# Re-ordering a memory-to-memory quadrant swap: one DMA engine per neighbouring row, steps of 4 MB, one queue

## The chip, the cores and the metric

The kernel runs on one core of a Trainium2 chip. The metric is the device time of one execution in microseconds (us). "Before" is the tuned kernel, "after" the changed one. A ratio is the mean time of one kernel's fast runs over the mean time of the other's fast runs in the same rounds, so it is not quite the ratio of the medians that are quoted with it. An interval is a 95% interval.

Some words: DMA (direct memory access) engines are the 16 units that move the data. A transfer is what one instruction orders; it goes into a queue and is carried out in packets, here one contiguous piece by one engine. It has landed when all its packets are written, which a semaphore, a counter that can be waited for, reports. On a profile page each digit of the DMA line is the busy share of the engines in one fortieth of the span, in tenths (9 is 90% or more), and the GB/s line is the rate in the same fortieths.

## The reference

```python
"x": np.random.randn(8192, 8192).astype(np.float32)     # 256 MB
return np.fft.ifftshift(x)
```

With even sizes this swaps the quadrants: the upper left one with the lower right one, the upper right one with the lower left one. No value is computed. A row is 32 KB, half a row 16 KB, a quadrant 4096 half rows.

## The kernel before

```python
STEP = 8
...
    dims = [[STEP * C, hr // STEP], [1, hc]]
    for c in range(STEP):
        for col in (0, hc):
            for eng, r0, h in ((nc.sync, 0, col), (nc.scalar, hr, hc - col)):
                eng.dma_start(
                    out=bass.AP(out.tensor, out.offset + (r0 + c) * C + h, dims),
                    in_=bass.AP(x.tensor, x.offset + (hr - r0 + c) * C + hc - h, dims),
                )
```

There are 32 transfers of 8 MB, straight from memory to memory: 512 half rows each, every eighth row of a quadrant. A transfer is split over 16 DMA engines, 32 rows each, so the engines stand 8 MB apart and each walks in steps of 256 KB. Two queues, the sync engine's and the scalar engine's, each get 16 transfers.

## Time and profile before

| | before |
|---|---|
| time, median of 3 | 811.38 us (811.26 to 811.44) |
| span of the first profile | 821.3 us |
| half-row packets of 16 KB | 16,384, mean 801 ns in that profile |
| fastest packets | 611 ns |

The profiled execution of 821.3 us does not belong to the timed ones of 811.4 us. A later set of runs offers an explanation: of five chips on record four give about 811 us, but one gave 822.47 us for this very kernel (median of 9, 821.90 to 823.20), and the first profiled execution took 823.08 us.

To read such a page: there are no compute rows worth looking at. What matters is the busy line (are there holes?), the rate line (is there one regime or several?) and the packet durations in the trace (how long does 16 KB keep one engine?).

### The profile page before, as it was taken

What the parts mean: (1) busy time and instruction counts of PE and PEld (TensorE: products, weight loads), DVE (VectorE), ACT (ScalarE), POOL (GpSimd) and SP (SyncE); (2) the same over time, 40 slices, a digit from 0 to 9 for tenths busy, and PEclk for the clock granted to TensorE, in tenths of its full rate; (3) what the DMA queues carried; (4) which work ended last, traced back from release to release, by engine and by line L of the source; (5) the groups of instructions that cost most, each with busy time, mean ns of one, the idle gap of its engine ahead of it and who ended that gap; (6) DMA issues with size and microseconds to landing.
All of it is one profiled execution on the core that took longest, in us unless ns stands there. A gap on an engine that the chain in (4) does not pass through costs nothing. (4 is left out here: it accounts for less than half of the span.)

```text
span 821.3 us, 77 instructions
## 1 busy us (share of the span) xinstructions
POOL 0.2 (0%) x4
## 2 busy tenths in 40 slices
POOL 0000000000000000000000000000000000000000
DMA  9999999999999999999999999999999999999998
GB/s 304 325 328 333 326 325 330 321 329 330 325 330 330 327 328 333 329 330 330 328 328 327 334 325 330 326 326 328 331 329 330 326 332 326 328 324 333 326 328 298
DMA packets 16896, 268.44 MB, mean 327 GB/s; under 512 B 512, under 2 KB 512, under 8 KB 512
## 3 DMA queue, kind: packets, MB, share of 16 engines
q1 hardware_dynamic: 8448, 134.22, 50.2%
q10 hardware_dynamic: 8448, 134.22, 49.7%
HBM read 268.44 MB, written 268.44 MB: 654 GB/s over the span
## 5 line engine op out<-in xcount | busy, mean ns | idle before, releaser
L51 POOL MEMSET const-bfloat16-1.0<- 128x1 bf16 x1 | 0.1, 103 | 0.0
L51 POOL MEMSET const-uint8-127<- 128x1 uint8 x1 | 0.1, 102 | 0.0
L51 POOL MEMSET const-float32-0.0<- 128x1 f32 x1 | 0.1, 99 | 0.2 <-issue 0.2
L51 POOL MEMSET const-float32-1.0<- 128x1 f32 x1 | 0.1, 99 | 0.0
## 6 DMA issues: line engine op xcount, KB each, us to landing
out_dram<-in_x_dram ACTq DMA_DIRECT2D x16, 8192.0 KB, 204.3
out_dram<-in_x_dram SPq DMA_DIRECT2D x16, 8192.0 KB, 204.1
```

The source lines that it names most:

```text
L51: nc = _bacc.Bacc("TRN2", target_bir_lowering=False, num_devices=1)
```

## The change

The intent is to keep the 16 engines out of each other's way: at any moment they work on 16 neighbouring rows, one each, and move on together by 128 rows (4 MB). Eight passes with other residues fill a quadrant. All transfers go through one queue.

```diff
-STEP = 8
+ENGINES = 16
+POSITIONS = 8
...
-    dims = [[STEP * C, hr // STEP], [1, hc]]
-    for c in range(STEP):
+    stride = POSITIONS * ENGINES
+    dims = [[C, ENGINES], [stride * C, hr // stride], [1, hc]]
+    for r0 in (0, hr):
         for col in (0, hc):
-            for eng, r0, h in ((nc.sync, 0, col), (nc.scalar, hr, hc - col)):
-                eng.dma_start(
-                    out=bass.AP(out.tensor, out.offset + (r0 + c) * C + h, dims),
-                    in_=bass.AP(x.tensor, x.offset + (hr - r0 + c) * C + hc - h, dims),
+            for p in range(POSITIONS):
+                row = p * ENGINES
+                nc.sync.dma_start(
+                    out=bass.AP(out.tensor, out.offset + (r0 + row) * C + col, dims),
+                    in_=bass.AP(x.tensor, x.offset + (hr - r0 + row) * C + hc - col, dims),
                 )
```

Three things change at once: which engine touches which row, the number of queues, and the order of the quadrants.

## The prediction

> **What bounds the kernel now.** The kernel has no arithmetic: it copies four quadrants of a 256 MB matrix from memory to memory. So I read the page from the DMA side only: first the busy line and the rate line in 40 slices, then the queue totals, then the issues, then who waits on the issuing queues.
>
> ```profile
> DMA  9999999999999999999999999999999999999998
> GB/s 304 325 328 333 326 325 330 321 329 330 325 330 330 327 328 333 329 330 330 328 328 327 334 325 330 326 326 328 331 329 330 326 332 326 328 324 333 326 328 298
> DMA packets 16896, 268.44 MB, mean 327 GB/s; under 512 B 512, under 2 KB 512, under 8 KB 512
> ...
> q1 hardware_dynamic: 8448, 134.22, 50.2%
> q10 hardware_dynamic: 8448, 134.22, 49.7%
> HBM read 268.44 MB, written 268.44 MB: 654 GB/s over the span
> ```
>
> The reader is to see three things. The 16 DMA engines are busy in every slice, so there is no gap to close: time can only come out of how long one packet takes. The rate is flat, so there is one regime and not several stages. And each byte is counted twice at the memory: 268.44 MB read and the same written, 654 GB/s together.
>
> The 512 small packets are completion writes (32 transfers by 16 engines); the other 16,384 are half rows of 16 KB. The trace keeps start, duration and queue of each. Their mean duration is 801 ns and their sum over 16 engines 820 us, so packets fill the engines from first to last. Their distribution is the most telling fact: over a quarter stand at 611 ns (25th percentile 611, median 773, 90th 1046, 99th 1298). So 611 ns, 16,384 B at 26.8 GB/s per engine, is the pace of an engine that nothing delays, and the mean packet spends 190 ns over that. All 1,024 packets of each engine at 611 ns would be 626 us; the difference to 820 is delay in the memory or on the way to it.
>
> The issues are not the limit:
>
> ```profile
> out_dram<-in_x_dram ACTq DMA_DIRECT2D x16, 8192.0 KB, 204.3
> out_dram<-in_x_dram SPq DMA_DIRECT2D x16, 8192.0 KB, 204.1
> SPq L33 <- DMA out_dram<-in_x_dram: 133.8, 12, 50.6
> ```
>
> 204 us from issue to landing is eight transfers' worth: one takes 818 / 32 = 25.6 us of the engines' time, and eight semaphores are in rotation, four per queue. The 133.8 us on the third line are the sync queue waiting for one of its semaphores to come free, with several transfers still queued. The earliest issues, which met empty rings, took 0.6 to 0.9 us against the 25.6 us that a transfer lasts. Issue is 30 times faster than it has to be.
>
> One more view matters, the rate in chosen stretches (columns: microseconds, GpSimd, clock, DMA share, GB/s):
>
> ```profile
> 5.00:13.00 8.00, 0.00 (x0) 1.00 1.03 360
> ...
> 21.00:40.00 19.00, 0.00 (x0) 1.00 1.01 329
> ...
> 400.00:410.00 10.00, 0.00 (x0) 1.00 1.02 334
> ```
>
> In the first 8 us after the start-up the kernel moved about 350 to 360 GB/s. In the packet records these are ten rounds in which all 16 engines run in step, each packet 715 to 880 ns, none at 611, a new round every 744 ns on average (262,144 B / 744 ns = 352 GB/s). Then the engines fall out of step, durations spread from 611 to 1,500 ns, and the rate settles at 329. So contention among the 16 streams, not the total alone, costs the last 7%.
>
> **What the Trainium skill says.** "HBM Reference", section Specifications (TRN2), gives about 716 GB/s for a memory domain. The trace agrees with it as a ceiling: 654 GB/s over the span is 91% of it, and the in-step stretch, 2 x 352 = 704, is 98%. "DMA: Bandwidth & Descriptors", section Why a DMA increments its semaphore by 16 and not by 1, says that a transfer is split over the largest number of engines up to 16 that divides its slowest dimension. The trace agrees as far as it can: 16 completions per transfer (256 small packets per queue, 16 transfers). The same page, section Latency and other measured facts, reports that copies of tiles with rows of 16 KiB at a pitch of 4 or 8 MiB ran at 103 GB/s where padded ones had 214, and calls aliasing of lock-stepped streams an inference. This trace does not agree simply: neighbouring engines are now 8 MB apart and yet reach 91% of the ceiling. The same page, section Issuing engines are not separate DMA queues, says that a second issuing engine saves only issue time; the trace has that at 0.6 to 0.9 us.
>
> **The change part by part.**
>
> 1. Which engine touches what. Before: a transfer's slowest dimension is 512 rows at 8 rows (256 KB) pitch, split over 16 engines by 32 rows each. Engines are 32 x 256 KB = 8 MB apart, and each walks in steps of 256 KB. After: the slowest dimension is 16 neighbouring rows, so engines are 32 KB apart and each walks 32 rows in steps of 128 rows = 4 MB. Bytes, packet size (16 KB) and number of packets stay: 16,384. Cost by count: none. Its effect is all in the mean packet, 801 ns now. At 744 ns (the in-step stretch) the engines would need 1,024 x 744 = 762 us in place of 820; that is 58 us in the profiled run, 7%. This is the most I expect: it is also 98% of the skill's ceiling.
>
> 2. One queue. 32 transfers still; all from the sync engine. Issue: 32 x 0.9 = 29 us at most, spread over 800 us, all hidden. Three transfers per queue went out before an issue stalled at the start, so a single queue should hold some 3 x 25 = 75 us of work ahead. One queue alone can feed the engines: the first rounds of the trace are the sync queue's alone, and their packets took 611 and 662 ns. No gain, no loss by itself. What it does change is that at one time only one quadrant is read and one is written; today two pairs are interleaved packet by packet.
>
> 3. Order of quadrants. Now one queue writes left half rows while the other writes right half rows, so both halves are read and written at once. After, for 16 transfers at a stretch only one half row is read and only the other written (16 KB apart within the 32 KB row). If the memory spreads 16 KB pieces unevenly this could help or hurt; no view tells.
>
> Sum: 0 of issue, 0 of bytes, between -58 us and an unknown positive amount from the memory. I take a quarter to a third of the possible gain, about 15 us.
>
> **The rivals.** (a) The memory is the bound whatever the order: 654 of 716 GB/s with reads and writes mixed is already high, and the short in-step stretch is a start-up effect (writes lagging reads). For it: the rate is flat over 800 us through very different row positions, and the mean packet by position within a transfer hardly moves (748 to 850 ns, without a trend). Then 800 to 820 us. (b) Aliasing of steps: if each engine's own 4 MB step is what the skill's 103 GB/s come from, and not the distance among engines, the kernel slows; halved it would be 1,600 us, but milder forms, 850 to 950, are likelier, since 16 engines now lie in 16 different places of half a megabyte. Against it: padding by 4 KiB cured the skill's case, which spreads the streams in the low address bits, as 32 KB between engines does here. (c) The neighbours stay out of each other's way at any time, as no two engines ever share the low bits of a row number within a pass: the in-step rate holds for the whole run. 811.38 x 329 / 352 = 758 us. (d) The single queue leaves bubbles between packets: against it, the 611 ns packets of the first rounds.
>
> **Range and chances.** (a) is the likeliest single course, some 40%; (c), wholly or in part, some 35%; (b) and (d) together some 25%. Middle: 796 us, 811.4 less the 15 above. The range of 8 in 10 runs from a nearly full gain, 760, to a mild slowdown, 850. Chances: faster by over 2% (under 795) 0.37, within 2% 0.38, slower 0.25.
>
> **What would show it.** Step 1 is right if the mean of the 16 KB packets falls below 801 ns towards 744 and the rate line rises from 327 towards 350; wrong if the spread of packet durations stays as it is (a) or its upper tail grows beyond 1,300 ns (b). Step 2 is right if all packets stand on one queue, the busy line keeps its nines and landing stays near eight transfers' worth; holes in the busy line would show (d). Step 3 shows as a jump in the rate line halfway through each half of the span, where the column changes. The prediction fails most badly if the memory punishes a 4 MB step as the skill's tiles were punished.

## The result, and the profile after

| | before | after |
|---|---|---|
| time, median of 3 | 811.38 us (811.26 to 811.44) | 819.18 us (819.11 to 821.43) |
| ratio | | 1.0105 (1.0079 to 1.0132) |

The time hardly moves: the kernel is 1% slower, with an interval that leaves out 1.00. Executions over 1.5% slower than the fastest of the same kernel are left out of the means. These are the lines of the page of after that answer to those that the prediction shows of before:

```profile
DMA  9999999999999999999999999999999999999998
GB/s 300 331 326 333 330 337 330 331 330 332 325 333 331 333 324 333 329 331 330 329 326 338 331 327 327 328 334 332 327 330 339 326 329 333 326 325 334 332 326 292
DMA packets 16896, 268.44 MB, mean 328 GB/s; under 512 B 512, under 2 KB 512, under 8 KB 512
...
q1 hardware_dynamic: 16896, 268.44, 99.3%
HBM read 268.44 MB, written 268.44 MB: 657 GB/s over the span
...
out_dram<-in_x_dram SPq DMA_DIRECT2D x32, 8192.0 KB, 107.7
```

All packets stand on one queue; the busy line has kept its nines; the rate line is as flat as before, with no jump where the half row changes. From issue to landing it is now 107.7 us, some four transfers' worth. Semaphores are not the reason: the trace shows eight in rotation in both kernels. What changed is how much waits in the queues. On one queue the first three issue instructions took 0.6 to 0.7 us, but the median of all 32 is 24.6 us, about the time of one transfer. So the sync engine stands in the issue itself, presumably until there is room in the queue (argued from these times), with about four transfers under way. Two queues had eight. Engines that are always busy do not notice.

There is a trap here. This page says 657 GB/s and the first page of before says 654, as if the change had gained. The two pages come from different executions, and the timed runs say the opposite. So I ran both kernels again on one chip. The first fence is before, the second after:

```profile
GB/s 307 335 332 332 334 329 336 334 332 332 333 336 332 334 334 333 328 335 336 333 333 333 334 331 331 332 330 333 333 332 334 336 331 336 333 329 334 333 334 299
DMA packets 16896, 268.44 MB, mean 331 GB/s; under 512 B 512, under 2 KB 512, under 8 KB 512
...
HBM read 268.44 MB, written 268.44 MB: 663 GB/s over the span
```

```profile
GB/s 302 328 333 327 327 329 324 334 334 333 329 336 335 325 331 334 323 335 331 328 334 327 335 322 339 327 335 332 334 327 331 327 330 334 328 329 327 331 336 286
DMA packets 16896, 268.44 MB, mean 329 GB/s; under 512 B 512, under 2 KB 512, under 8 KB 512
...
HBM read 268.44 MB, written 268.44 MB: 657 GB/s over the span
```

Now the order is right: 663 GB/s before, 657 after. The packet records say where the difference sits. The mean packet is 786.3 ns before and 792.8 ns after; times 1,024 packets per engine that is 6.7 us, and the spans differ by 816.8 - 809.9 = 6.9 us. The floor of 611 ns has not moved; the upper tail has grown (95th percentile 1,059 to 1,134 ns, 99th 1,206 to 1,378). So in this pair the loss is a little more waiting inside packets, over the whole run, and nothing is left for issue or for the ends. The mean alone is not sharp enough to rest on: in the profile of b1_pairing below, a kernel that is nearly as slow as after, it is only 788.8 ns, and the rest lies between the packet records. The upper tail is the steadier mark, as will be seen.

### The profile page after: what moved, and what is told of

Its sections match the earlier page's. It is cut to its first block, busy times and chain, and to the rows that moved or that the text cites. A ratio compares the mean times of both kernels' runs of the same rounds, so it can differ in the third digit from the quotient of the medians.

```text
span 817.3 us, 77 instructions
## 1 busy us (share of the span) xinstructions
POOL 0.2 (0%) x4
## 6 DMA issues: line engine op xcount, KB each, us to landing
out_dram<-in_x_dram SPq DMA_DIRECT2D x32, 8192.0 KB, 107.7
```

## The experiments

The theory of the prediction (call it C) was that contention among the 16 streams takes 7% from the copy and that a better row order wins some of it back. Its main rival (M) was that the memory bounds reads and writes together, whatever the order. For the 1% of loss there were four suspects: the single queue (Q), the 4 MB step (S), engines on neighbouring rows (N), the order of half rows (H).

### Noise, and the queue alone

Four kernels ran on one chip. The first is before itself.

> The kernel before against itself, to size the noise. If the 811.4 us and the 823 us of its profiled execution are two samples of one spread, its runs here scatter between 811 and 823 and the ratio's interval is about 1% wide around 1.00. If the profile itself adds the 1.4%, the timed runs stay within 0.1% of 811.4 and only the profiled one is at 823.

Measured: 811.58 us (811.45 to 812.04) against 811.27 us, ratio 1.0004 (0.9992 to 1.0016). A ratio of 1.01 is thus far outside the noise. The profiled execution took 811.72 us, so profiling adds nothing; the guess that the profile costs 1.4% is dead.

The second is after, repeated.

> The changed kernel again on the same chip. Theory M (the memory bounds both orders alike): ratio 1.00 to 1.01, mean packet within 2% of before's. Theory L (a real loss of 1% from the new layout or the single queue): ratio 1.008 to 1.013 again, with an interval that leaves out 1.00.

Measured: 819.37 us (818.51 to 821.29), ratio 1.0103 (1.0089 to 1.0116). The loss is real.

The third undoes everything but the queue:

```diff
-            for eng, r0, h in ((nc.sync, 0, col), (nc.scalar, hr, hc - col)):
+            for eng, r0, h in ((nc.sync, 0, col), (nc.sync, hr, hc - col)):
```

> Only the queue part of the change: the rows of before, all 32 transfers on the sync engine's queue. Theory Q (the single queue costs the 1%): ratio 1.01, as the changed kernel. Theory M: ratio within 0.5% of 1.00; busy line keeps its nines and landing falls from 204 to some 105 us as in the changed kernel, since four transfers are in flight.

Measured: 811.69 us (810.48 to 811.78), ratio 1.0004 (0.9991 to 1.0016), mean packet 787.6 ns. The single queue costs nothing. Q is out.

The fourth keeps the new rows but gives neighbouring passes to two queues in turn:

```diff
-                nc.sync.dma_start(
+                (nc.sync, nc.scalar)[p % 2].dma_start(
```

> Only the row part of the change: 16 neighbouring rows, 4 MB steps, neighbouring passes on the sync and the scalar engine's queues in turn. Theory Q: the time of before, ratio 1.00. Theory that the 4 MB steps cost it: ratio 1.01 as the changed kernel. Theory M: within 0.5% of 1.00.

Measured: 822.73 us, ratio 1.0142 (1.0109 to 1.0174), with a wide scatter (817.69 to 828.71). The loss goes with the rows, not with the queue, and two passes side by side may make it larger (the intervals of the two ratios overlap). Why the scatter is wide I did not find out.

### Which part of the new row order

All four of the next kernels use one queue. The first takes the quadrants in before's order:

```diff
-    for r0 in (0, hr):
+    for p in range(POSITIONS):
+        row = p * ENGINES
         for col in (0, hc):
-            for p in range(POSITIONS):
-                row = p * ENGINES
+            for r0, h in ((0, col), (hr, hc - col)):
```

> The rows of the changed kernel, but the order of quadrants of before: transfers alternate between the two quadrant pairs, so both half rows are read and written within every 50 us. Theory H (reading one half row and writing the other for 16 transfers costs the 1%): ratio to before 1.000 to 1.003. Theory S (the 4 MB step) and theory N (engines on neighbouring rows): ratio 1.008 to 1.014 as for the changed kernel.

Measured: 818.54 us, ratio 1.0085 (1.0071 to 1.0098). H explains little or nothing of it.

The second makes the step small, 512 KB, and keeps the neighbours:

```diff
-    dims = [[C, ENGINES], [stride * C, hr // stride], [1, hc]]
+    dims = [[C, ENGINES], [ENGINES * C, hr // stride], [1, hc]]
...
-                row = p * ENGINES
+                row = p * (hr // POSITIONS)
```

> 16 neighbouring rows at a time as in the changed kernel, but each engine steps by 512 KB, a plain sweep through the quadrant. Theory S: back to before, 1.000 to 1.003. Theory N: 1.010 as the changed kernel. Theory H: 1.010 as well.

Measured: 817.00 us, ratio 1.0065 (1.0053 to 1.0078). Most of the loss stays (b1_pairing, with neighbours and 4 MB steps on the same chip, has 1.0085, and the two intervals overlap).

The third makes the step large, 16 MB, in transfers of 2 MB:

```diff
-POSITIONS = 8
+POSITIONS = 32
```

> The changed kernel with steps of 16 MB: 8 rows per engine and transfer, 128 transfers of 2 MB. Theory S: the loss is as large or larger, 1.010 to 1.03, and the 99th percentile of the packets rises over the changed kernel's 1378 ns. Theory N and H: 1.010, with the same packets. If the smaller transfers cost anything it shows as holes in the busy line.

Measured: 816.45 us, ratio 1.0058 (1.0044 to 1.0072). A larger step does not make it worse, which speaks against S.

The fourth keeps the 4 MB step and parts the engines, eight rows (256 KB) from each other:

```diff
-    dims = [[C, ENGINES], [stride * C, hr // stride], [1, hc]]
+    dims = [[POSITIONS * C, ENGINES], [stride * C, hr // stride], [1, hc]]
...
-                row = p * ENGINES
+                row = p
```

> Steps of 4 MB as in the changed kernel, but the engines 8 rows (256 KB) apart instead of on neighbouring rows. Theory S: 1.010 or more. Theory N: 1.000 to 1.003. Theory H: 1.010.

Measured: 811.15 us (810.59 to 811.37), ratio 0.9995 (0.9982 to 1.0007); the 99th percentile of the packets is back at 1,188 ns. This kernel has the 4 MB step, the single queue and the new order of half rows, and no loss. So N is the cause: the engines stand on neighbouring rows. On the chips of 811 us the 99th percentile agrees in every profile of a correct copy in 16 KB pieces without restarts: 1,338 to 1,381 ns in the six with neighbouring rows (both of after, a4, b1, b2, b3), 1,188 to 1,206 in the four without (a1, a3, b4 and d2 below). That the loss is 0.6% with steps of 512 KB and 16 MB and 0.9 to 1.0% with 4 MB stays unexplained.

### How far apart is far enough, and is it the reads or the writes

```diff
-    dims = [[C, ENGINES], [stride * C, hr // stride], [1, hc]]
+    dims = [[2 * C, ENGINES], [stride * C, hr // stride], [1, hc]]
...
-                row = p * ENGINES
+                row = p // 2 * 2 * ENGINES + p % 2
```

> The changed kernel with the engines two rows (64 KB) apart instead of one. If only direct neighbours disturb each other: ratio to before 0.998 to 1.002. If the loss fades with distance: about 1.005. If 64 KB is as bad as 32 KB: 1.009 to 1.012.

Measured: 810.73 us (810.51 to 811.56), ratio 0.9994 (0.9982 to 1.0006). With the engines on every second row the 1% is gone. The loss does not fade out over a longer distance: it is there at 32 KB and gone at 64 KB.

Two kernels use the near rows on one side only and rows 256 KB apart on the other. Their outputs are wrong, which doesn't matter for the times.

```diff
+    near = [[C, ENGINES], [stride * C, hr // stride], [1, hc]]
+    far = [[POSITIONS * C, ENGINES], [stride * C, hr // stride], [1, hc]]
...                                   # reads near, writes far; and the mirror
+                rrow, rdims, wrow, wdims = p * ENGINES, near, p, far
```

> One queue, 4 MB steps; the 16 engines read neighbouring rows (32 KB apart) but write rows 256 KB apart, a wrong result on purpose. If neighbouring reads cause the loss: ratio to before 1.007 to 1.012. If neighbouring writes do: 0.998 to 1.002. If both share: near 1.005.

> The mirror: reads 256 KB apart, writes on neighbouring rows, a wrong result on purpose. If neighbouring writes cause the loss: 1.007 to 1.012. If neighbouring reads do: 0.998 to 1.002. If both share: near 1.005.

Measured, on the slower chip where before itself takes 822.47 us: reads near 825.11 us, ratio 1.0031 (1.0017 to 1.0044); writes near 827.61 us, ratio 1.0064 (1.0051 to 1.0076). Both sides share, the writes with about twice the weight, and 0.31% + 0.64% is nearly the whole 1.0%. After itself was not run on this chip, so that the two losses add up to its loss is argued, not shown.

### Is there a faster regime to be had

First the ceiling. Two kernels move the same 16,384 pieces of 16 KB one way only, between memory and on-chip buffers. Their outputs are wrong, which doesn't matter for the times.

```diff
# reads only
+    pool = ctx.enter_context(tc.tile_pool(name="sb", bufs=8))
...
+                    t = pool.tile([P, hc], mybir.dt.float32)
+                    nc.sync.dma_start(out=t[:], in_=bass.AP(x.tensor, ..., dims))
# writes only: one tile t, to all half rows
+                    nc.sync.dma_start(out=bass.AP(out.tensor, ..., dims), in_=t[:])
```

> Only the reads: all half rows into on-chip buffers, almost nothing written to memory, so the result is wrong on purpose. Same 16,384 pieces of 16 KB. Theory M (memory reads and writes together are the bound, some 665 GB/s): the packets stand at the engines' own pace, 611 ns, and the time is about 1024 x 0.611 + 8 = 634 us. Rival R (the reads alone are already limited at some 330 GB/s): about 811 us.

> Only the writes: one on-chip tile written to all half rows, a wrong result on purpose. Theory M: packets at 611 ns, about 634 us. Rival W (writes alone are limited at some 330 GB/s, and the reads ride along): about 811 us.

Measured: 639.04 us (638.75 to 639.27) and 640.89 us (640.83 to 640.96), mean packets 615 and 617 ns. The rate lines, reads first, then writes:

```profile
GB/s 373 429 429 428 428 429 428 428 428 428 428 428 428 428 428 428 430 430 432 429 429 427 428 429 429 428 428 430 428 428 428 428 429 428 428 428 428 428 429 332
```

```profile
GB/s 328 427 427 427 427 427 427 427 427 427 427 427 427 427 427 427 427 427 427 427 427 426 427 428 427 427 427 428 427 430 428 427 427 429 428 427 427 427 428 385
```

The reader is to see lines without a ripple: alone, neither side is delayed much, and both run close to the 611 ns of the fastest packets of the copy. Only together, at 2 x 331 = 662 GB/s, does waiting appear. (These two runs also move between memory and on-chip buffers instead of memory and memory, in transfers of 2 MB with the engines 2 MB apart; that this alone changes nothing was not tested. So it is not shown whether the memory itself or the path to it sets the 662 GB/s.)

Then the start. The prediction had read ten quick rounds at the start of the trace as a regime that contention ends. This kernel starts all engines together 32 times, with before's rows and one queue:

```diff
+    sem = ctx.enter_context(nc.semaphore())
+    with tc.tile_critical():
...
+                    ).then_inc(sem, 16)
+                    n += 16
+                    nc.sync.wait_ge(sem, n)
```

> The rows of before on one queue, with a wait for each transfer's landing before the next is issued, so all 16 engines start in step 32 times. Prediction's own reading (the in-step stretch is a faster regime that contention ends): each restart gives some 10 rounds at 744 ns and no repayment, so the busy time of a transfer falls by 0.4 us and more against 25.2 us, and the whole is 811 + 32 x (2 to 3 us of empty pipes). Rival (start-up effect, reads running ahead of writes, repaid at once): ten fast rounds, then rounds above 800 ns, and the sum over a transfer is no less than in steady flow. Either way the time is some 880 us; the packet records tell them apart.

Measured: 874.85 us, ratio 1.078 (1.0764 to 1.0796). The busy line has the holes of 31 restarts:

```profile
DMA  9989998889988899888999899998899898999988
...
q1 hardware_dynamic: 16896, 268.44, 91.5%
```

The waits of the sync queue in the same run (who, for whom, us in total, times, longest):

```profile
SPq L36 <- DMA out_dram<-in_x_dram: 827.3, 31, 26.9
```

The sync queue stands 26.9 us for a landing at the longest, in place of queueing ahead. Worked out from the packet records: sort a transfer's 512 packets by start and take every sixteenth; the steps between these, averaged over the 32 transfers, are

```
round      1-5  about 1030, 683, 606, 609, 635 ns
round      6-12 about 719 741 743 741 742 742 754 ns
round     13-20 about 775 792 845 830 825 839 856 820 ns
round     21-31 about 780 767 804 814 783 789 796 789 805 752 800 ns
```

All 32 transfers have the same quick stretch, about 740 ns per round in rounds 6 to 12 (the stretch that the prediction built on), and in all 32 it is followed at once by slow rounds: rounds 13 to 20 take 823 ns on average (802 to 845 in the single transfers), more than the 786 ns of steady flow (the run on one queue, above); rounds 6 to 20 together average 784 ns. So this stretch is no regime that could last, and it is repaid.

The still quicker rounds before it are not repaid in this list: all 31 steps add up to 24.0 us, and 31 x 786 ns would be 24.4. The mean packet says the same, 780.1 ns against 787.6. That lies between the two readings of the expectation: 0.24 us less busy time per transfer, where the prediction's own reading asked for 0.4 and more, and the rival's for none. But each start has its cost too. The first packets take 1,119 ns on average, and from first packet to last end a transfer takes 25.57 us here, against 805.5 / 32 = 25.17 us in steady flow. By starting anew nothing is won. What is filled in the quick rounds and emptied later no record shows; that reads run ahead of writes is only argued.

### Is 811 us a floor for this copy

Whole rows, halves not swapped: the same bytes in half as many pieces. Its output is wrong, which doesn't matter for the time.

```diff
+    dims = [[STEP * C, hr // STEP], [1, C]]
```

> Whole rows of 32 KB moved between the upper and lower half, without swapping left and right, a wrong result on purpose: the same bytes in half as many pieces, and no half rows. Theory M: within 0.5% of 811 us. Rival (half rows leave the memory something to gain): below 795 us.

Measured: 812.64 us (812.35 to 813.50), ratio 1.0015 (1.0002 to 1.0028). The mean packet of 32 KB takes 1,578.6 ns, 789 per 16 KB. Longer pieces win nothing.

Pieces of 4 KB, with the engines 256 KB apart:

```diff
+    W = 1024
-    dims = [[POSITIONS * C, ENGINES], [stride * C, hr // stride], [1, hc]]
+    dims = [[POSITIONS * C, ENGINES], [stride * C, hr // stride], [1, W]]
+                for w in range(0, hc, W):
```

> The best order so far (engines 256 KB apart, 4 MB steps, one queue), each half row cut into four pieces of 4 KB in four transfers. Theory M (the sum of memory traffic is the bound): within 1% of 811 us, mean packet near 197 ns. Rival (the delay is one collision per piece or the piece's size sets it): clearly different, by over 2%.

Measured: 894.92 us (883.00 to 904.80), ratio 1.0947 (1.0907 to 1.0986); its profile fell in a slow run, so the rate is only roughly read from it:

```profile
DMA  9999999999999999999999999999999999999997
GB/s 285 320 308 315 289 295 310 287 312 284 298 317 281 315 289 302 315 286 311 287 301 313 295 310 288 295 317 286 316 283 305 311 287 317 287 302 313 288 311 244
```

The expectation of M was missed. The engines are busy all through, yet the rate swings between 281 and 320. More than half of the packets take 159 ns (four make 636, hardly over 611), but a tenth take 396 ns and more. The number of transfers is not the reason: b3_step_16m has 128 of 2 MB as well, and lost only its 0.6%. So the 811 us hold for pieces of 16 and 32 KB, not for this copy in 4 KB pieces. Whether the size of the pieces does it, or that an engine now jumps 4 MB after every 4 KB, was not separated.

### Can the place of the streams matter more than 1%

Before's rows on one queue, but each engine reads its first half row 32 times. Its output is wrong, which doesn't matter for the time.

```diff
-    dims = [[STEP * C, hr // STEP], [1, hc]]
+    odims = [[32 * STEP * C, 16], [STEP * C, 32], [1, hc]]
+    idims = [[32 * STEP * C, 16], [0, 32], [1, hc]]
```

> The copy on one queue with the rows of before, but each engine reads its first half row 32 times, a wrong result on purpose. Reads then touch 16 pieces per transfer instead of 512. If the order and place of the reads set the delay, the time falls clearly below 811 us, towards 762 or 634. If the path or the total of traffic sets it, it stays within 1% of 811.

Measured: 1960.75 us (1939.73 to 1972.52), ratio 2.41.

```profile
DMA  9999999999999999999999999999999999999999
GB/s 134 136 138 134 140 137 133 136 136 138 137 135 137 139 138 134 138 142 133 132 143 136 139 135 139 134 135 136 139 133 137 135 138 135 138 133 136 139 140 132
```

Neither expectation foresaw this. The busy line is as full as ever at less than half the rate, which is the best lesson on that line: busy is not fast. The same with the engines on neighbouring rows:

```diff
-    idims = [[32 * STEP * C, 16], [0, 32], [1, hc]]
+    idims = [[C, 16], [0, 32], [1, hc]]
```

(and the rows of the output as in after).

> The repeated reads again (each engine reads one half row 32 times, a wrong result on purpose), but with the engines on neighbouring rows instead of 8 MB apart. If reads 8 MB apart collide with each other, the time falls from 1961 us to about 811. If repeating one place is slow in itself, it stays near 1961.

Measured: 815.64 us, ratio 1.0053 (1.0035 to 1.0070). So repeating one place is not slow in itself (the writes of this kernel differ too, but those of the slow one are those of before, which cost nothing there). Sixteen reads that stay 8 MB apart collide heavily; the same engines 8 MB apart that move on by 256 KB after each piece, as in before, lose nothing that any order here wins back.

## Why the prediction was wrong

It foresaw 796 us; the result is 819.18 us. The time is inside the range, which 760 to 850 owes to its width, and the class "within 2%" was given 0.38, but the direction is wrong, and so is its reason.

**The step that failed** is part 1: "At 744 ns (the in-step stretch) the engines would need 1,024 x 744 = 762 us", of which it took "a quarter to a third of the possible gain, about 15 us". The 744 ns were measured right (though single packets of that stretch lasted 669 to 879 ns, not 715 to 880) but were not a regime. In 32 restarts out of 32 these rounds were followed by rounds of 802 to 845 ns, 823 on average, and from first packet to last end a transfer was no shorter for them. And no order that was tried gains anything: before, the 256 KB distance and the 64 KB distance all end at 811 us (ratios 0.9994 to 1.0004). The 58 us were too many in any case: they start from the 801 ns of the slower first profile; from the 786 ns of the chips of 811 us it would have been 1,024 x (786 - 744) ns = 43 us. The +7 us that stand in place of the -15 us come from neighbouring rows (6.5 ns per packet, 1,024 packets per engine), which the prediction had counted as an advantage.

**Point by point.** That the engines have no gap, and that only the mean packet can move the time, was right: 6.7 of 6.9 us. Part 2, one queue without gain or loss, was right (ratio 1.0004); that landing stays at eight transfers' worth was wrong, it halved, without effect (part 2's own "some 3 x 25 = 75 us of work ahead" had it nearly right, and contradicts the sign that the prediction then gave). Part 3 left open whether half rows matter; they do not by more than about 0.2%. Rival (a), the memory bounds whatever the order, comes nearest for the size of the result: reads and writes alone run at 615 and 617 ns a packet, together they stop at 663 GB/s. Its guess of "800 to 820" held; "whatever the order" did not (+1% here, a factor of 2.41 for the fixed reads), and that it is the memory is not shown. Rival (b), that the 4 MB step aliases, is refuted by the kernel with 256 KB distance (0.9995). Its sign came true all the same, an upper tail beyond 1,300 ns (99th percentile 1,378): the neighbouring rows make it too, so the sign could not tell the two apart. Rival (c), that neighbours keep out of each other's way, is refuted outright: distance, not nearness, is what helps. Rival (d), bubbles of the single queue, is refuted.

**What stays open:** what inside the memory makes rows 32 KB apart disturb each other, why the loss depends on the step, and why 663 GB/s and not more is the end for both directions together, in the memory or on the way to it.

No kernel here beats before by more than the noise; the best correct ones, 810.73 and 811.15 us, equal it.

## What to carry to other kernels

Before you extrapolate a quick stretch at the start of a trace, look at the stretch right after it: here rounds of 740 ns were followed by rounds of 823 ns, and only a sum over both is a rate. Measure reads alone and writes alone before you work on the order of a copy: where both run near the engines' own pace and only together do not, as here, the order may have little to give, and here no order that was tried gave anything. Two cost something: concurrent streams on directly neighbouring rows (0.6 to 1.4%), and reads that stay 8 MB apart without moving (a factor of 2.41). Compare profiles of one chip only; the same program differed by 1.4% between two chips, more than the effect that was looked for.

## What the Trainium skill lacked or had wrong

- "HBM Reference", Specifications (TRN2), gives 716 GB/s for a domain. No page says how much of it a copy from memory to memory by one core can reach; the one rate of such a copy is in the row on pitch of the next point. Here it is 663 GB/s (93% of 716), 331 each way, on the chips where before takes 811 us, and some 1.4% less on the slower chip (822 us).
- "DMA: Bandwidth & Descriptors", Latency and other measured facts, has 103 GB/s per direction at row pitches of 4 and 8 MiB, and calls 214 the full rate. The 331 GB/s each way seen here are well above that full rate. And a pitch alone does not decide, though no run here has that row's shape (128 rows, each 4 or 8 MiB from the next; the prediction set it beside the 8 MB between the engines of before, whose rows are 256 KB apart): steps of 4 MB cost nothing when the engines are 64 KB or 256 KB apart (0.9994, 0.9995), engines 8 MB apart cost nothing while they move by 256 KB (811 us), and cost a factor of 2.41 when their reads stay in place. The opposite case is missing there: engines on rows 32 KB apart lose 0.6 to 1.4%.
- No page has the cost of piece size for such a copy: 32 KB and 16 KB pieces are nearly equal (ratio 1.0015), 4 KB pieces, each 4 MB from the engine's last one, cost 9.5%.
